# A chunked recurrence in a four-layer block: five elementwise steps moved to GpSimd, the 16x16 inverse built from two 8x8 ones, one root per group, and another order of the pieces

## The chip, the cores and the metric

The kernel runs on one core of a Trainium2 chip. The core has five engines that run side by side, each with an instruction queue worked off in order: TensorE (PE; its weight loads are shown apart as PEld), VectorE (DVE), ScalarE (ACT), GpSimd (POOL) and SyncE (SP, which issues most DMAs). Engines wait for each other by semaphores only. The metric is the device time of one execution in microseconds, lower is better.

## What is computed

One sequence of 512 tokens, width 1024, goes through four layers: a recurrent mixer (RWKV-7), windowed attention, a gated spatial unit and gated linear attention, each followed by a gated feed-forward block, everything in float32. The change touches the first mixer alone. Its core, per head (16 heads of 64 columns):

```python
def step(state, inp):
    r_t, d_t, k_t, v_t, kk_t, a_t = inp
    sa = jnp.einsum('bhvk,bhk->bhv', state, kk_t)
    state = (state * d_t[:, :, None, :]
             - sa[..., None] * (kk_t * a_t)[:, :, None, :]
             + v_t[..., None] * k_t[:, :, None, :])
    return state, jnp.einsum('bhvk,bhk->bhv', state, r_t)
...
mean = jnp.mean(y, -1, keepdims=True)
var = jnp.mean(jnp.square(y - mean), -1, keepdims=True)
y = ((y - mean) * lax.rsqrt(var + RW_GN_EPS)).reshape(B, S, D) * gn_g + gn_b
bonus = (jnp.sum(hs(r) * hs(k) * r_k, -1, keepdims=True) * hs(v)).reshape(B, S, D)
return ((y + bonus).astype(x.dtype) * g) @ w_o
```

## The kernel before

**How it is put in order.** The kernel's code does not emit instructions; every call is recorded as an operation with a price (`price`), and a planner (`Program.run`) then hands the operations out greedily, engine by engine, inside a window of 700 recorded operations, earliest recorded first unless another can start much sooner. The result is one fixed order per engine. The planner also counts PE's work and, where PE would otherwise rest too long, puts in filler products of the identity with itself (line 525 of the profile). All real instructions carry line 239, the planner's `call`, so they are told apart by their tiles. What is recorded first, and at what price, thus sets the order; `ORDERS` says in which sequence the pieces of the recurrence are recorded.

**The recurrence.** It is done in chunks of 64 tokens (eight of them), in four groups of two column blocks of 128 (four heads a group). Each group goes through these pieces:

- *prepare* (`rwkv_prepare`, pieces `f` and `q`): decays by a scan over tokens, keys, receptances. It writes `qk` (what is multiplied by the state) and `kb` (what goes into it), whose tiles are called `qk`, `h` or `rk` according to the group; temporaries are `ew` and `et` (`slot` for the first group). Two of its steps are `kn * kf[p]` (tile `ew<-ew,rk`) and the outer part of `qk`, receptance times decay (`qk<-rk,et` and alike).
- *products* (`rwkv_products`, first half of the pieces `p`): the 64x64 products of keys with keys and receptances per chunk and head, masked on their way out of PSUM into `pr` or `pa`; beside it `kb` is multiplied by the chunk's whole decay `pend`.
- *inverse* (`rwkv_inverse`, the other pieces `p`): 64x64 triangular blocks are inverted. ACT collects their 16x16 diagonal blocks on the partitions (`et` or `slot`), DVE turns them by a 32x32 transpose, solves column by column (15 steps, each a product and a sum over the last axis, of i*i elements in step i), and turns back. Two levels of PE products, ACT masks (`low`) and DVE transposes and sums (`mt`) then make 32x32 and 64x64 inverses (`iv`). `rwkv_direct` folds them into `qk`.
- *chain* (`rwkv_chain`, pieces `c`): four blocks of two chunks. In each chunk PE multiplies `qk` by the state `st`, ACT copies the result (`vu`), PE makes the chunk's contribution to the state, and DVE adds it to the decayed state (`st<-ps,wu`, two halves). This is serial from chunk to chunk. Each second block ends with ACT's copy of `y` (tile `out`).
- *out* (`rwkv_out`, pieces `o`, one for each half of the tokens): mean, variance and `rsqrt` (eleven small DVE instructions, tiles `gvar`, `grs`, `rs_t`), the bonus on POOL (`out<-v,bonus`), transposes, gate, and the split for the output projection.

The pieces of group n's chain are recorded between those of the inverse of group n + 1 and the preparation of later groups. `pr` and `pa` have one buffer each, so the products of group n + 2 wait for the chain of group n. The first group's preparation and inverse are recorded beside the projection of the values (PE `whi,slot` and `wlo,slot`, dense work); the output projection (`et,rk`) follows the last group, and its first part is done beside it. From there on PE is dense through the rest of the program. The lines of the inverse's steps:

```python
for i in range(1, 16):
    w = tmp[:, :i * i].rearrange("p (j m) -> p j m", j=i)
    nc.vector.tensor_mul(w, n1[:, i, :i].unsqueeze(1).to_broadcast([P, i, i]), t4[:, 0, :i, :i])
    nc.vector.tensor_reduce(t4[:, 0, :i, i], w, axis=AX.X, op=ALU.add)
nc.scalar.copy(t4[:, 1], t4[:, 0])
nc.vector.transpose(n, tt)
```

Of the kernel before, what the change touches and what calls it, by code (L numbers as in the profile page):

```python
# [29 lines left out]
ALSO = {"exp": ("tanh",), "sigmoid": ("tanh",), "silu": ("sin", "tanh"), "gelu": ("tanh",)}  # L30
ORDERS = "ffppcpqcpqqcopcopcoo", "ppcpqcpqqcopcopcoo", "ppcpcpcopcopcoo", "cccococ"
LOCAL = "qqqqqaqaqaqaoaoooaoaoaoo"
# [474 lines left out]
class K:  # L507
# [509 lines left out]
    def rwkv(self, g, g_next, slots):  # L1017
# [5 lines left out]
        nc, d = self.nc, self.d  # L1023
# [14 lines left out]
        v = self.v = self.load_cols()  # L1038
# [197 lines left out]
    def part(self, name, dt=F32, w=S):  # L1236
        p = self.pl[name]
        return p.tile([P, w], dt, name="slot" if p is self.big else name)

    def rwkv_prepare(self, sb, rf, kf, twa, keep, sel, rs, ka1):  # L1240
# [18 lines left out]
        for i, p in enumerate(sb['pairs']):  # L1259
# [41 lines left out]
    def rwkv_products(self, sb, hf):  # L1301
# [6 lines left out]
        for i in range(2):  # L1308
# [12 lines left out]
    def rwkv_inverse(self, sb):  # L1321
# [16 lines left out]
        nc.vector.transpose(n, zx)  # L1338
        n2, t4 = n.rearrange("p (t b m) -> p t b m", t=16, b=2), tt.rearrange("p (j b i) -> p b j i", j=16, b=2)
        n1 = zx[:, :256].rearrange("p (t m) -> p t m", t=16)  # L1340
# [140 lines left out]

    def rwkv_out(self, sb, hf, y, tg):

        nc = self.nc
        H, W = 8, 256
        hd = lambda t: t.rearrange("p (h c) -> p h c", h=H)
        bc = lambda t, n=H: t.unsqueeze(2).to_broadcast([P, n, 64])
        mean, var, rs = [self.sm.tile([P, H], F32, name=n) for n in ("gmean", "gvar", "grs8")]
        sq, bv = self.part("out"), self.part("out")
        for j in range(2):  # L1490
            b = hf * 2 + j
            bo = sb['bonus'][:, b].rearrange("p g h -> p (g h)")
            four = lambda t: t.rearrange("p (h c) -> p h c", h=4)
            nc.gpsimd.tensor_mul(four(bv[:, j * W:(j + 1) * W]), four(sb['v'][b]), bc(bo, 4))
        nc.vector.tensor_reduce(mean, hd(y), axis=AX.X, op=ALU.add)
        nc.vector.tensor_scalar(mean, mean, 1.0 / 64, None, op0=ALU.mult)
        nc.vector.tensor_sub(hd(y), hd(y), bc(mean))
        nc.scalar.activation(sq, y, AF.Square)
        nc.vector.tensor_reduce(var, hd(sq), axis=AX.X, op=ALU.add)
        nc.vector.tensor_scalar(var, var, 1.0 / 64, 64e-5, op0=ALU.mult, op1=ALU.add)  # L1500
        self.rsqrt(rs, var)
        nc.vector.tensor_mul(hd(y), hd(y), bc(rs))
        yt, bt, gt = [self.bank() for _ in range(3)]
# [499 lines left out]
def consts():  # L2003
# [10 lines left out]
    f = np.arange(S)  # L2014
    eye = np.broadcast_to((f // 32 == f % 16).astype(np.float32), (P, S)).copy()
    return {'rw_masks': masks, 'rw_eye': eye, 'rope_freq': freq}
# [129 lines left out]
```

## Time and profile before

| what | us |
|---|---|
| median of three runs (2392.96 to 2395.63) | 2394.17 |
| profiled execution, first to last instruction (its span) | 2393.6 |
| PE busy in it | 2352.7 |
| DVE busy in it | 1934.0 |
| ACT busy in it | 1437.0 |
| POOL busy in it | 326.3 |

The profiled execution is one of its own; its span of 2393.6 us stands 0.6 us below the median of the runs, and no other time is known of it. Times inside the program are counted from its first instruction. PE's busy time includes the time that a product takes from start to end, also where a next one could start earlier, so a busy PE is not one at its peak. "Idle before, released by" names the instruction whose semaphore came last.

The first group's inverse ends at about 205 us, the chains of the four groups end at about 256, 304, 350 and 391 us, and the output projection ends at about 431 us.

### The profile page before, as it was taken

Reading aid. Unit: us, or ns where it says so; the run is one execution under the profiler, and the core shown is the slowest. Engines: PE = TensorE matmul, PEld = TensorE weight load, DVE = VectorE, ACT = ScalarE, POOL = GpSimd, SP = SyncE. Lnnn points to the kernel's source line nnn. Section 1 sums busy time; section 2 is a strip of 40 time slices with the busy share of each in tenths; the row PEclk is TensorE's granted clock in tenths of the full one; section 3 lists DMA queues with packets and bytes.
Section 4 is the critical chain, followed back from the end, with each engine's and each line's share of the span. In section 5 each row is a group of like instructions: output and inputs, shape, how many; then the busy total and the mean of one; then the engine's idle time right before and its main releaser. Section 6 shows DMA issues by size and latency. Waiting matters only on the chain.

```text
span 2393.6 us, 36634 instructions
## 1 busy us (share of the span) xinstructions
PE 2352.7 (98%) x13524; PEld 1925.6 (80%) x13524; DVE 1934.0 (81%) x3261; ACT 1437.0 (60%) x2514; POOL 326.3 (14%) x398
## 2 busy tenths in 40 slices
PE   9999889999999999999999999999999999999998
PEld 8577777988888769888887888888888778988886
DVE  8577987887889878878699888886869978886868
ACT  4476765755556587555575444755557737755555
POOL 0000000221211001211111101121121101121110
PEclk9999999999999999999999999999999999999999
DMA  5220012998998326999988664899898758899985
GB/s 174 71 77 13 8 66 65 214 217 221 220 213 202 88 65 156 211 234 217 215 217 212 187 157 100 197 210 227 219 216 210 166 134 171 203 204 233 218 207 118
DMA packets 127603, 404.23 MB, mean 169 GB/s; under 512 B 14400, under 2 KB 17984, under 8 KB 127424
## 3 DMA queue, kind: packets, MB, share of 16 engines
q0 software_dynamic: 51840, 176.18, 41.2%
q1 hardware_dynamic: 75584, 225.72, 28.1%
q8 instruction: 106, 1.74, 0.3%
q14 instruction: 73, 0.60, 0.1%
HBM read 397.39 MB, written 2.10 MB: 167 GB/s over the span
## 4 chain that ended last, share of the span: by engine, by line
PE 83%; DVE 6%; ACT 5%; DMA 4%; issue 2%; SPq 0%; POOL 0%; DVEq 0%; ACTq 0%; POOLq 0%
PE ps L239 83%; DVE slot L239 2%; ACT slot L239 2%; DMA wraw<-ffn_w_a 2%; DMA wraw<-ffn_w_b 1%; DVE wlo L239 1%; ACT et L239 1%; ACT whi L239 1%; DVE h L239 1%; ACT vu L239 0%; ACT wu L239 0%; DMA wraw<-sg_w_o 0%; ACT L239 0%; DVE left L239 0%; DMA slot<-x 0%
## 5 line engine op out<-in xcount | busy, mean ns | idle before, releaser
L239 PE MATMUL ps<-whi,slot 128*128 128x512 f32 (+1 forms) x5072 | 1554.2, 384 | 3.6 <-DVE slot L239 3.1
L239 PEld LDWEIGHTS ps<-whi,slot 128*128 128x128 f32 x5072 | 943.3, 188 | 179.2 <-ACT whi L239 8.0
L239 ACT CAST whi<-wraw 128x1024 fp32r<-128x1024 f32 (+3 forms) x843 | 688.3, 836 | 565.4 <-PE ps L239 432.9
L239 DVE TENSOR_TENSOR wlo<-wraw,whi 128x1024 fp32r<-128x1024 f32 (+3 forms) x843 | 790.5, 954 | 256.6 <-ACT whi L239 254.8
L239 PE MATMUL ps<-wlo,slot 128*128 128x512 f32 (+1 forms) x2536 | 968.9, 382 | 1.8 <-DVE wlo L239 1.8
L239 PEld LDWEIGHTS ps<-wlo,slot 128*128 128x128 f32 x2536 | 476.5, 188 | 86.5 <-DVE wlo L239 6.6
L239 PE MATMUL ps<-slot,whi 128*128 128x512 f32 x688 | 217.1, 395 | 1.0 <-ACT slot L239 1.0
L239 DVE TENSOR_TENSOR slot<-ps,slot 128x512 f32<-128x512 f32 (+2 forms) x271 | 161.0, 608 | 48.4 <-PE ps L239 33.9
L239 ACT CAST slot<-left 128x512 fp32r<-128x512 f32 (+1 forms) x294 | 164.6, 589 | 53.4 <-PE ps L239 29.5
L239 DVE TENSOR_TENSOR slot<-left,slot 128x512 fp32r<-128x512 f32 (+1 forms) x294 | 183.4, 644 | 10.8 <-ACT slot L239 6.9
L239 DVE TENSOR_TENSOR h<-h,ps 128x512 f32<-128x512 f32 x240 | 159.7, 683 | 27.7 <-PE ps L239 25.2
L239 POOL DMA_DIRECT2D wraw<-ffn_w_a x128 | 109.7, 860 | 497.8 <-DVE wlo L239 415.1
L239 PEld LDWEIGHTS ps<-slot,whi 128*128 128x128 f32 x688 | 127.7, 188 | 32.7 <-DVE slot L239 2.6
L239 PE MATMUL ps<-slot,wlo 128*128 128x512 f32 x344 | 133.9, 391 | 0.0
L239 POOL DMA_DIRECT2D wraw<-ffn_w_b x64 | 54.9, 864 | 419.9 <-DVE slot L239 119.9
L239 ACT COPY slot<-ps 128x512 f32<-128x512 f32 (+1 forms) x144 | 78.4, 562 | 39.0 <-PE ps L239 36.9
L239 POOL DMA_DIRECT2D wraw<-ffn_o_a x64 | 54.6, 853 | 285.6 <-DVE wlo L239 151.9
L239 ACT COPY left<-ps 128x512 f32<-128x512 f32 x108 | 54.8, 558 | 57.0 <-PE ps L239 57.0
L239 PE MATMUL ps<-ident,slot 128*128 128x128 f32 x561 | 85.8, 277 | 0.9 <-DVE slot L239 0.6
L239 PEld LDWEIGHTS ps<-ident,slot 128*128 128x128 f32 x561 | 63.3, 140 | 26.0 <-DVE slot L239 12.9
L239 PEld LDWEIGHTS ps<-slot,wlo 128*128 128x128 f32 x344 | 64.5, 188 | 14.2 <-DVE wlo L239 0.8
L239 DVE SCALAR_TENSOR_TENSOR slot<-slot,ncol 128x512 f32<-128x512 f32 (+1 forms) x96 | 65.1, 701 | 9.2 <-ACT slot L239 9.0
(302 smaller groups left out, 2070.2 us busy)
## 6 DMA issues: line engine op xcount, KB each, us to landing
wraw<-ffn_w_a SPq DMA_DIRECT2D x128, 512.0 KB, 6.6
wraw<-ffn_w_a POOLq DMA_DIRECT2D x128, 512.0 KB, 6.9
wraw<-ffn_o_a SPq DMA_DIRECT2D x64, 512.0 KB, 5.1
wraw<-ffn_o_a POOLq DMA_DIRECT2D x64, 512.0 KB, 7.3
wraw<-ffn_w_b SPq DMA_DIRECT2D x64, 384.0 KB, 3.9
wraw<-ffn_w_b POOLq DMA_DIRECT2D x64, 384.0 KB, 6.4
wraw<-gla_w_p SPq DMA_DIRECT2D x24, 512.0 KB, 4.9
wraw<-gla_w_p POOLq DMA_DIRECT2D x24, 512.0 KB, 6.3
```

What stands on the lines that cost most here:

```text
L239: op = self.add(eng.name, lambda: getattr(eng.target, what)(*map(real, args), **{k: real(a) for k, a in kw.items()}), *self.price(eng.name ...
```

## The change

Five products leave DVE for POOL: `kn * kf[p]`, the outer part of `qk`, the decay of `kb`, and the subtraction of the mean (two, two, four and two instructions a group). The 16x16 solve becomes two 8x8 solves in one (seven steps over both diagonal blocks), then two 512-element products with a sum each for the block below; ACT's copy now writes both transposed copies, 512 elements, and the table of ones that starts the solve has another layout. For the first three groups both halves of the tokens share one root; the last group keeps one for each half. The strings in `ORDERS` are permuted.

```diff
-ORDERS = "ffppcpqcpqqcopcopcoo", "ppcpqcpqqcopcopcoo", "ppcpcpcopcopcoo", "cccococ"
+ORDERS = "ffppcpqpqqccopcpocoo", "ppcpqcqppqcocopcoo", "pcpcppcpcoopcoo", "ccccooc"
...
-            out = (self.rwkv_out(sb, hf, sb['y'][hf], tg) for hf in range(2))
+            out = self.rwkv_norm(sb, tg, ((0, 1),) if n < 3 else ((0,), (1,)))
...
-            nc.vector.tensor_mul(kn, kn, kf[p])
+            nc.gpsimd.tensor_mul(kn, kn, kf[p])
...
-            nc.vector.tensor_mul(outer(qk), nat(rf[p]), nat(e))
+            nc.gpsimd.tensor_mul(outer(qk), nat(rf[p]), nat(e))
...
-            nc.vector.tensor_mul(kb, kb, sb['pend'][:, i, hf * 4:hf * 4 + 4].unsqueeze(2).to_broadcast([P, 4, P]))
+            nc.gpsimd.tensor_mul(kb, kb, sb['pend'][:, i, hf * 4:hf * 4 + 4].unsqueeze(2).to_broadcast([P, 4, P]))
...
-        for i in range(1, 16):
-            w = tmp[:, :i * i].rearrange("p (j m) -> p j m", j=i)
-            nc.vector.tensor_mul(w, n1[:, i, :i].unsqueeze(1).to_broadcast([P, i, i]), t4[:, 0, :i, :i])
-            nc.vector.tensor_reduce(t4[:, 0, :i, i], w, axis=AX.X, op=ALU.add)
-        nc.scalar.copy(t4[:, 1], t4[:, 0])
-        nc.vector.transpose(n, tt)
+        for i in range(1, 8):
+            w = n[:, :2 * i * i].rearrange("p (q j m) -> p q j m", q=2, j=i)
+            nc.vector.tensor_mul(w, nq[:, :, i, :i].unsqueeze(2).to_broadcast([P, 2, i, i]), tq[:, :, :i, :i])
+            nc.vector.tensor_reduce(tq[:, :, :i, i], w, axis=AX.X, op=ALU.add)
+        w = n.rearrange("p (j i m) -> p j i m", j=8, i=8)
+        eights = [P, 8, 8, 8]
+        nc.vector.tensor_mul(w, n1[:, 8:, :8].unsqueeze(1).to_broadcast(eights), t1[:, :8, :8].unsqueeze(2).to_broadcast(eights))
+        nc.vector.tensor_reduce(x1, w, axis=AX.X, op=ALU.add)
+        nc.vector.tensor_mul(w, t1[:, 8:, 8:].rearrange("p m i -> p i m").unsqueeze(1).to_broadcast(eights), x1.unsqueeze(2).to_broadcast(eights))
+        nc.vector.tensor_reduce(t1[:, :8, 8:], w, axis=AX.X, op=ALU.add)
+        nc.scalar.copy(tmp.rearrange("p (j b i) -> p j b i", j=16, b=2), t1.unsqueeze(2).to_broadcast([P, 16, 2, 16]))
+        nc.vector.transpose(n, tmp)
...
+    def rwkv_norm(self, sb, tg, turns):
...
+        for turn in turns:
+            var, rs = [self.sm.tile([P, 2 * H], F32, name=n)[:, :H * len(turn)] for n in ("gvar", "grs8")]
...
+                nc.vector.tensor_reduce(mean, hd(y), axis=AX.X, op=ALU.add)
+                nc.vector.tensor_scalar(mean, mean, 1.0 / 64, None, op0=ALU.mult)
+                nc.gpsimd.tensor_sub(hd(y), hd(y), bc(mean))
+                nc.scalar.activation(sq, y, AF.Square)
+                nc.vector.tensor_reduce(part(var, j), hd(sq), axis=AX.X, op=ALU.add)
+                if hf != turn[-1]:
+                    yield
+            nc.vector.tensor_scalar(var, var, 1.0 / 64, 64e-5, op0=ALU.mult, op1=ALU.add)
+            self.rsqrt(rs, var)
+            for j, hf in enumerate(turn):
+                nc.vector.tensor_mul(hd(sb['y'][hf]), hd(sb['y'][hf]), bc(part(rs, j)))
+                self.rwkv_out(sb, hf, tg)
+            yield
```

What moves on the engines: every engine's order is the same up to the first group's preparation and again from the output projection on; between them it is planned anew. PE, at the end of the value projection, where the first group's levels begin (`slot,pa` and `slot,low` are the two levels of its inverse, `h` the next group's products, L525 the fillers), before:

```order
L239 MATMUL ps<-whi,slot 128x512
L239 MATMUL ps<-ident,qk 128x128 x4
L239 MATMUL ps<-ew,sel 32x128 x4
L239 MATMUL ps<-h 128x128 x12
L525 MATMUL ps<-ident 128x128 x4
L239 MATMUL ps<-slot,pa 64x64 x32
L525 MATMUL ps<-ident 128x128 x2
L239 MATMUL ps<-slot,low_1209 64x64 x16
L239 MATMUL ps<-slot,low_1224 64x64 x16
L525 MATMUL ps<-ident 128x128 x4
L239 MATMUL ps<-slot,pa 64x64 x32
```

and now:

```order
L239 MATMUL ps<-wlo,slot 128x512
L239 MATMUL ps<-whi,slot 128x512
L239 MATMUL ps<-slot,pa 64x64 x32
L239 MATMUL ps<-whi,slot 128x512
L239 MATMUL ps<-slot,low_1209 64x64 x16
L239 MATMUL ps<-slot,low_1224 64x64 x16
L239 MATMUL ps<-wlo,slot 128x512
L239 MATMUL ps<-whi,slot 128x512
L239 MATMUL ps<-ew,sel 32x128 x4
L239 MATMUL ps<-h 128x128 x3
L239 MATMUL ps<-slot,pa 64x64 x32
```

The fillers are gone from there, the last value products and the next group's products stand between the levels. DVE, at the end of the second group's solve, before:

```order
L239 TENSOR_TENSOR et<-et 128x196
L239 TENSOR_TENSOR ew<-ew,rk 128x512
L239 TENSOR_REDUCE et<-et 128x14
L239 TENSOR_TENSOR rk<-ew,et 128x4x2x64
L239 TENSOR_TENSOR et<-et 128x225
L239 SCALAR_TENSOR_TENSOR ew<-rk,vec,ew 128x512
L239 TENSOR_REDUCE et<-et 128x15
L239 TENSOR_TENSOR rs_t<-grs_2440 128x8
L239 TENSOR_TENSOR st_1175<-ps,wu 64x2x64
```

and now:

```order
L239 TENSOR_TENSOR et<-et 128x98
L239 TENSOR_TENSOR st_1197<-ps,wu 64x2x64
L239 TENSOR_REDUCE et<-et 128x2x7
L239 TENSOR_TENSOR et<-et 128x512
L239 TENSOR_REDUCE gmean<-out 128x8
L239 TENSOR_REDUCE et<-et 128x64
L239 TENSOR_TENSOR st_1175<-ps,wu 64x2x64
L239 TENSOR_TENSOR et<-et 128x512
L239 TENSOR_TENSOR st_1175<-ps,wu 64x2x64
L239 TENSOR_REDUCE et<-et 128x8x8
```

The long tail of growing steps has become two pairs of 512 elements, and the chain's additions still stand between the steps. POOL, in the second and third group, had the bonus alone before:

```order
L239 TENSOR_TENSOR out<-v_1360,bonus 128x256
L239 TENSOR_TENSOR out<-v_1375,bonus 128x256
L239 TENSOR_TENSOR out<-v_1421,bonus 128x256
L239 TENSOR_TENSOR out<-v_1435,bonus 128x256
L239 TENSOR_TENSOR out<-v_1666,bonus 128x256
```

and now:

```order
L239 TENSOR_TENSOR ew<-ew,rk 128x512
L239 TENSOR_TENSOR out<-out,gmean 128x512
L239 TENSOR_TENSOR rk<-rk,pend 128x512 x4
L239 TENSOR_TENSOR out<-v_1362,bonus 128x256
L239 TENSOR_TENSOR out<-v_1376,bonus 128x256
L239 TENSOR_TENSOR out<-v_1424,bonus 128x256
L239 TENSOR_TENSOR out<-v_1438,bonus 128x256
L239 TENSOR_TENSOR qk<-rk,et 128x4x2x64
L239 TENSOR_TENSOR out<-out,gmean 128x512
L239 TENSOR_TENSOR ew<-ew,rk 128x512
```

Forty instructions of 512 elements have joined POOL's queue, which works them off in order. ACT's queue has one table load (`ACT_TABLE_LOAD`) more, at the last group's preparation.

More of the change, by code (lines that the diff above doesn't have):

```diff
@@ L1338, in rwkv_inverse @@
         nc.vector.transpose(n, zx)
[L1339 to L1340 removed]
+        n2 = n.rearrange("p (t b m) -> p t b m", t=16, b=2)
+        n1, t1, x1 = [t.rearrange("p (t m) -> p t m", m=m) for t, m in ((zx[:, :256], 16), (tt[:, :256], 16), (tt[:, 272:336], 8))]
         nc.vector.tensor_add(n1, n2[:, :, 0, :], n2[:, :, 1, :])
[L1342 to L1347 removed]
+        nq, tq = [t[:, :272].rearrange("p (q x) -> p q x", q=2)[:, :, :P].rearrange("p q (t m) -> p q t m", t=8) for t in (zx, tt)]
+        for i in range(1, 8):
[10 more added lines that the diff above has]
+        nc.vector.transpose(n, tmp)
         tu = n.rearrange("p (j x u) -> p u x j", j=16, x=2)
@@ L1480, in rwkv_chain @@
             yield
-    def rwkv_out(self, sb, hf, y, tg):
+    def rwkv_norm(self, sb, tg, turns):
         nc = self.nc
-        H, W = 8, 256
+        H = 8
         hd = lambda t: t.rearrange("p (h c) -> p h c", h=H)
-        bc = lambda t, n=H: t.unsqueeze(2).to_broadcast([P, n, 64])
-        mean, var, rs = [self.sm.tile([P, H], F32, name=n) for n in ("gmean", "gvar", "grs8")]
-        sq, bv = self.part("out"), self.part("out")
+        bc = lambda t: t.unsqueeze(2).to_broadcast([P, H, 64])
+        for turn in turns:
+            var, rs = [self.sm.tile([P, 2 * H], F32, name=n)[:, :H * len(turn)] for n in ("gvar", "grs8")]
+            part = lambda t, j: t[:, j * H:(j + 1) * H]
+            for j, hf in enumerate(turn):
+                y, sq, mean = sb['y'][hf], self.part("out"), self.sm.tile([P, H], F32, name="gmean")
+                nc.vector.tensor_reduce(mean, hd(y), axis=AX.X, op=ALU.add)
[7 more added lines that the diff above has]
+            self.rsqrt(rs, var)
+            for j, hf in enumerate(turn):
+                nc.vector.tensor_mul(hd(sb['y'][hf]), hd(sb['y'][hf]), bc(part(rs, j)))
+                self.rwkv_out(sb, hf, tg)
+            yield
@@ L1490, in rwkv_out @@
+    def rwkv_out(self, sb, hf, tg):
+        nc, y = self.nc, sb['y'][hf]
+        W = 256
+        bv = self.part("out")
         for j in range(2):
-            b = hf * 2 + j
-            bo = sb['bonus'][:, b].rearrange("p g h -> p (g h)")
             four = lambda t: t.rearrange("p (h c) -> p h c", h=4)
-            nc.gpsimd.tensor_mul(four(bv[:, j * W:(j + 1) * W]), four(sb['v'][b]), bc(bo, 4))
-        nc.vector.tensor_reduce(mean, hd(y), axis=AX.X, op=ALU.add)
-        nc.vector.tensor_scalar(mean, mean, 1.0 / 64, None, op0=ALU.mult)
@@ L1497, in rwkv_out @@
[L1497 to L1502, printed above, removed]
+            bo = sb['bonus'][:, hf * 2 + j].rearrange("p g h -> p (g h)")
+            nc.gpsimd.tensor_mul(four(bv[:, j * W:(j + 1) * W]), four(sb['v'][hf * 2 + j]), bo.unsqueeze(2).to_broadcast([P, 4, 64]))
@@ L2014, in consts @@
     f = np.arange(S)
-    eye = np.broadcast_to((f // 32 == f % 16).astype(np.float32), (P, S)).copy()
+    eye = np.broadcast_to((f // 16 == f % 16).astype(np.float32), (P, S)).copy()
     return {'rw_masks': masks, 'rw_eye': eye, 'rope_freq': freq}
```

## The prediction

> **What bounds the kernel now.** The page comes first: PE is busy nearly all the time, so a change that adds no dense work can only save time where PE is not doing any.
>
> ```profile
> span 2393.6 us, 36634 instructions
> PE 2352.7 (98%) x13524; PEld 1925.6 (80%) x13524; DVE 1934.0 (81%) x3261; ACT 1437.0 (60%) x2514; POOL 326.3 (14%) x398
> ```
>
> Next the busy times by stretch, cut where the chains of the four groups end (columns after the stretch's length: PE, PEld, DVE, ACT, POOL, then the granted clock).
>
> ```profile
> 165.00:205.00 40.00, 39.16 (x450) 33.20 (x446) 29.26 (x66) 20.45 (x34) 2.37 (x4) 1.00 0.09 28
> 205.00:258.00 53.00, 47.51 (x689) 34.49 (x680) 47.50 (x120) 44.97 (x93) 0.00 (x0) 0.94 0.05 15
> 258.00:305.00 47.00, 40.91 (x688) 33.63 (x686) 43.87 (x124) 33.00 (x78) 2.58 (x4) 1.00 0.04 10
> 305.00:352.00 47.00, 41.53 (x823) 34.96 (x819) 39.10 (x119) 32.31 (x78) 4.82 (x8) 1.00 0.23 79
> 352.00:393.00 41.00, 40.47 (x610) 32.00 (x607) 30.45 (x77) 24.73 (x63) 0.00 (x0) 1.00 0.08 26
> ```
>
> The three stretches from 205 to 352, one for each of the first three chains (I call them loops), are the only ones where PE rests visibly: 17.05 of 147 us, and its weight loads, which leave out the tails of small products, fill only 103.1 us. DVE is busy 47.5, 43.9 and 39.1 us there, 130.5 of 147 (89%), more than any other engine does work. In the fourth stretch the output projection fills PE, so nothing in it can save much; what comes after is ordered as before. The saving must come from the three loops and from the end of the stretch before them.
>
> Who waits in the loops:
>
> ```profile
> PEld ps L239 <- ACT vu L239: 15.2, 19, 1.6
> PEld ps L239 <- DVE st L239: 4.6, 13, 1.0
> ```
>
> That is the serial chain: PE's weight loads wait for ACT's copy `vu` and for DVE's state. And the chain of waits followed back through the loops, by shares:
>
> ```profile
> by line: PE ps L239 39.4%; ACT et L239 13.1%; ACT vu L239 6.3%; ACT wu L239 6.2%; issue 4.0%; ACT ew L239 3.3%; ACT L239 2.6%; PE ps L525 2.6%; DVE out L239 2.6%; ACT out L239 2.3%; DVE st L239 2.3%; DVE et L239 2.2%; DVE pr L239 2.0%; DVE
> ```
>
> The two views disagree: by busy time DVE is the bound, on the chain of waits its named rows are 9.1%, and with all that is cut off (11.1%) at most 20%. So a microsecond of DVE saved is worth between 0.2 and 0.89 us. That span is the main doubt of this forecast.
>
> **First term: the end of the value projection.** PE before the loops, from the timeline:
>
> ```profile
> 193.06 1.16 PE L525 MATMUL ps<-ident 128*128 128x128 f32 x8
> 194.64 2.08 PE L239 MATMUL ps<-slot,pa 64*64 64x64 f32 x64 [0.42 <-DVE slot L239]
> 196.65 0.71 PE L525 MATMUL ps<-ident 128*128 128x128 f32 x4
> 197.29 2.08 PE L239 MATMUL ps<-slot,low 64*64 64x64 f32 x64
> 199.31 1.16 PE L525 MATMUL ps<-ident 128*128 128x128 f32 x8
> 200.88 2.08 PE L239 MATMUL ps<-slot,pa 64*64 64x64 f32 x64 [0.42 <-DVE slot L239]
> ```
>
> PE has nothing but fillers from 193.06 to 194.64, 196.65 to 197.29 and 199.31 to 200.88: 3.79 us. In the new order these three places hold value products and products `h`, which cost nothing extra. For that the first solve must end sooner, which the terms below give it (some 3 us of DVE). A third I leave for products that are themselves late: **-2.5 us** (between -3.8 and 0).
>
> **Second term: work that leaves DVE in the loops.** The moved instructions there:
>
> ```profile
> L239 DVE TENSOR_TENSOR ew<-ew,rk 128x512 f32<-128x512 f32 x5 | 3.4, 682 | 0.0
> L239 DVE TENSOR_TENSOR qk<-rk,et 128x512 f32<-128x512 f32 x2 | 1.4, 684 | 0.0
> L239 DVE TENSOR_TENSOR rk<-rk,et 128x512 f32<-128x512 f32 x2 | 1.4, 681 | 0.0
> L239 DVE TENSOR_TENSOR h<-rk,et 128x512 f32<-128x512 f32 x1 | 0.7, 680 | 0.0
> L239 DVE TENSOR_TENSOR rk<-rk,pend 128x512 f32<-128x512 f32 x4 | 2.7, 684 | 0.2 <-PE ps L239 0.2
> L239 DVE TENSOR_TENSOR qk<-qk,pend 128x512 f32<-128x512 f32 x4 | 2.7, 682 | 0.0
> L239 DVE TENSOR_TENSOR h<-h,pend 128x512 f32<-128x512 f32 x3 | 2.1, 688 | 0.3 <-PE ps L239 0.2
> L239 DVE TENSOR_TENSOR out<-out,gmean 128x512 f32<-128x512 f32 x5 | 3.4, 685 | 0.0
> ```
>
> 26 instructions, 17.8 us. The other 14 of the forty lie under dense PE work before 205 or after 352, and count for nothing: PE is busy 39.2 of 40 and 40.5 of 41 us there.
>
> The solve, in the loops (three groups), with two of its products and what a 512-element sum and a strided read cost:
>
> ```profile
> L239 DVE TENSOR_TENSOR et<-et 128x256 f32<-128x256 f32 (+15 forms) x48 | 12.5, 261 | 0.8
> L239 DVE TENSOR_REDUCE et<-et 128x1 f32<-128x1 f32 (+14 forms) x45 | 10.5, 234 | 0.4
> L239 DVE TENSOR_TENSOR et<-et 128x49 f32<-128x49 f32 x1 | 0.2, 204 | 0.0
> L239 DVE TENSOR_TENSOR et<-et 128x225 f32<-128x225 f32 x1 | 0.4, 398 | 0.0
> L239 DVE TENSOR_REDUCE gmean<-out 128x8 f32<-128x512 f32 x6 | 4.1, 678 | 0.0
> L239 DVE TENSOR_TENSOR mt<-et,mk 128x256 f32<-128x256 f32 x12 | 6.3, 588 | 0.0
> ```
>
> 49 and 225 elements at 204 and 398 ns give 150 + 1.1 n ns. Before: 23.0 us less three additions of 256 elements (0.43 each), 21.7, or 7.2 a group in 30 instructions. Now seven products of 2, 8, 18, 32, 50, 72 and 98 elements (280): 7 x 150 + 1.1 x 280 = 1.36 us; their sums at most as much; two sums of 512 at 0.68; one product at 0.68, and one that reads in steps of 16 elements. For that the row `mt<-et,mk` stands (steps of 32): 588 against 432 by the formula, 0.31 us more for 512 elements, 0.99. Together 5.75 us in 18 instructions: 1.45 us a group, 4.4 us in the loops.
>
> The root:
>
> ```profile
> L239 DVE TENSOR_TENSOR rs_t<-grs 128x8 f32<-128x8 f32 x15 | 2.7, 180 | 0.0
> L239 DVE SCALAR_TENSOR_TENSOR grs<-rs_t,grs 128x8 f32<-128x8 f32 x15 | 2.3, 155 | 0.0
> L239 DVE SCALAR_TENSOR_TENSOR rs_t<-gvar,rs_t 128x8 f32<-128x8 f32 x15 | 2.3, 152 | 0.1
> ```
>
> Five roots, 7.3 us, 1.46 each; the six of the first three groups become three: 4.4 us. Eight columns more cost 8 x 1.1 ns. DVE is thus relieved of 17.8 + 4.4 + 4.4 = 26.6 us.
>
> **Third term: what POOL takes back.** POOL's price, and the one place in the loops where DVE is held up beside it:
>
> ```profile
> 343.84 1.27 POOL L239 TENSOR_TENSOR out<-v,bonus 128x256 f32<-128x256 f32 x2 [14.03 <-PE ps L239]
> 343.93 0.71 DVE L239 TENSOR_TENSOR et<-et 128x169 f32<-128x169 f32 x1
> 344.56 0.57 DVE L239 TENSOR_TENSOR rs_t<-grs 128x8 f32<-128x8 f32 x1
> ```
>
> Two products of 256 elements take POOL 1.27 us, so one of 512 takes about 1.25, against 0.68 on DVE. 26 of them are 32.5 us in 147, beside the twelve of 256 (7.4 us) that it has: POOL is not full, but queues in order. The two DVE rows should take 0.34 (by the formula) and 0.18 us; they took 0.37 and 0.39 longer and ended as POOL's did. Both read two SBUF tiles, and so do POOL's. The stall is 0.76 us for the loops' twelve POOL instructions, 0.06 each. With instructions twice as long it is at least 0.13 us for each of the 26, 3.4 us; at most DVE stands for what is left of 1.25 us after a short instruction or two, 0.9, or 23.4 us. About half of DVE's instructions in the loops read two SBUF tiles, but the four on `pend` stand beside masks that read PSUM. I take 0.3, nearer the measured end: 8 us. The Trainium skill (SBUF — State Buffer, "Who interferes with whom") says that a VectorE instruction with two SBUF inputs and a GpSimd instruction that reads SBUF shut each other out for their whole length. These two rows agree; by that rule alone the stall would go towards the upper end, 23.4 us, and the second term would be all but gone.
>
> **Net.** Relief of DVE in the loops: 26.6 - 8 = 18.6 us. Between 0.2 and 0.89 I take 0.55, the middle, since neither view has the better claim: **-10.2 us**.
>
> **Small terms.** On ACT, in the loops:
>
> ```profile
> L239 ACT COPY et<-et 128x256 f32<-128x256 f32 x3 | 1.2, 406 | 1.7 <-DVE et L239 1.7
> L239 ACT ACT_TABLE_LOAD x4 | 5.1, 1283 | 0.1
> ```
>
> The copy stands between the solve and DVE's turn and grows from 256 to 512 elements: between 0 and 0.4 us more, I take 0.2 in each of three groups, **+0.6**. One table load more costs nothing while ACT rests 14 us in that loop; uncovered it would be 1.3. PE's clock has one hole in the loops:
>
> ```profile
> 226.00:230.00 4.00, 1.77 (x32) 1.18 (x33) 3.26 (x7) 3.88 (x10) 0.00 (x0) 1.00 0.00 0
> 230.00:237.00 7.00, 6.80 (x86) 5.10 (x82) 5.41 (x23) 6.01 (x16) 0.00 (x0) 0.51 0.00 0
> ```
>
> After 4 us with PE busy 1.77 the granted clock is 0.51 for 7 us, 3.4 us of clock lost. Whether the new order keeps this hole, closes it or adds others no row shows: -3.4 if it closes, +3.4 for each new one, 0 taken.
>
> The mean's subtraction and the shared root make each half's output later; nobody but the output projection waits for it, and its first products come a loop later. POOL's queue puts `ew<-ew,rk` and the receptances behind the `pend` products, which wait for PE; late next are DVE's `kb` and the products of the following group.
>
> **Sum.** -2.5 - 10.2 + 0.6 = -12.1 us, a span of 2381.5; with the 0.6 us by which the runs' median stands above the span, 2382.1. I give 2382. Likeliest range: coupling 0.2 with 0.9 of the first term gives -5.4, coupling 0.89 with the stall at 8 us -18.5: 2375 to 2389.
>
> **The rivals.** *DVE is the bound throughout:* its 89% and idle times of 3 to 8 us a loop speak for it, the chain's 20% against. With the low stall, 23.2 x 0.89 + 3.8 = 24.4 us less: 2370. *The serial chain sets the pace, and the relief turns into DVE's idle time:* the 15.2 us for `vu` speak for it; the first term and the longer copy are left, 2392. Three new holes in PE's clock beside the forecast's gain end there too: 10.2 of 12.1 us gone. *POOL's products come onto the path:* `kn * kf`, the receptances' decay, the `pend` products and the mean each have a waiting instruction behind them; if each of 26 shows its extra length (1.25 - 0.68) and DVE's stalls come to the upper 23.4 us, the sum is -2.5 - 0.55 x 3.2 + 0.6 + 26 x 0.57 = +11.1, 2405. It decides, slower by more than 0.2%, once 15 of the 26 are on the path. Against it: most prepare a later group.
>
> **How the numbers follow.** Some 0.2%, 4.8 us, is what a measurement of this kernel tells from no change: below 2389.4 is faster, above 2399 slower. Forecast 0.60, DVE throughout 0.14, chain sets the pace or clock holes 0.15, POOL on the path 0.11 (0.03 of it ends within 0.2%). Faster is 0.60 + 0.14 + 0.03 of the chain case = 0.77, same 0.12 + 0.03 = 0.15, slower 0.08. The range takes in DVE throughout and the chain case: 2369 to 2393.
>
> **What would show it.** Right: no L525 rows between the first group's levels; `et<-et` in the loops near 17 us instead of 23; DVE about 110 to 120 us over the three loops; fourth stretch unchanged near 41 us. The port: DVE products with two SBUF inputs, `rk<-et,ew` or `ew<-ew,et`, longer than 0.69 us by some tenths in the mean. Wrong: loops as long as before with DVE's idle grown (chain), a granted clock below 0.94 in a loop (holes), or PE and DVE waiting for POOL by several us (POOL on the path).

## The result, and the profile after

The changed kernel takes 2417.48 us (median of 2413.1 to 2419.31) against 2394.47 for the kernel before on the same chip: a ratio of 1.0093, 95% interval 1.0081 to 1.0104. By this ratio it is slower by 22.3 us (the two medians lie 23.0 apart; differences between runs go by the ratio from here on). 2382 was forecast, and slower had a chance of 0.08. Its profiled execution spans 2416.4 us.

Head of the page after:

```profile
span 2416.4 us, 36518 instructions
PE 2362.3 (98%) x13508; PEld 1933.0 (80%) x13508; DVE 1929.1 (80%) x3140; ACT 1439.1 (60%) x2515; POOL 378.3 (16%) x438
```

By stretch, cut at the ends of the four chains as before (columns: length, then PE, PEld, DVE, ACT, POOL, granted clock, and DMA):

```profile
165.00:205.00 40.00, 37.65 (x447) 30.80 (x443) 28.10 (x51) 22.36 (x35) 6.37 (x6) 1.00 0.08 28
205.00:271.00 66.00, 53.81 (x862) 42.39 (x862) 51.62 (x95) 48.86 (x102) 18.96 (x15) 0.90 0.04 12
271.00:325.00 54.00, 45.85 (x756) 37.05 (x756) 43.72 (x96) 33.49 (x78) 12.20 (x12) 1.00 0.03 10
325.00:367.00 42.00, 37.11 (x491) 29.86 (x492) 31.81 (x75) 28.67 (x70) 9.92 (x12) 0.88 0.24 84
367.00:407.00 40.00, 39.89 (x675) 31.08 (x674) 27.57 (x71) 24.08 (x61) 3.27 (x4) 1.00 0.07 24
```

The three loops take 162 us instead of 147. DVE works 127.2 us in them instead of 130.5, so its idle time has grown from 16.5 to 34.8 us. PE rests 25.2 instead of 17.1 us, and its clock is at 0.90 and 0.88 in two of the loops. The output projection ends at 447.8 instead of 430.8 us, 17.0 of the 22.8 us by which the span grew; the rest lies later (the clock is at half once more, 504 to 510 us).

What PE lost up to there can be told in two numbers. Before and after, from 165 us to the end of the output projection:

```profile
165.00:430.80 265.80, 246.87 (x3402) 197.81 (x3398) 222.79 (x560) 175.70 (x389) 11.65 (x18) 0.99 0.16 49
165.00:447.80 282.80, 254.57 (x3412) 203.38 (x3408) 217.29 (x447) 179.85 (x390) 53.66 (x52) 0.96 0.15 47
```

PE rests 18.9 us before and 28.2 after: +9.3. Where the trace has PE at half clock, half of its busy time is lost: 3.3 us before, 10.6 after: +7.3. Together 16.6 of 17.0. A third sum is what the planner's fillers take of PE, 12.1 us before and 10.5 after. The table below has the three sums for every run.

**DVE beside POOL.** The two engines in the second group's preparation, DVE first:

```profile
243.13 0.62 DVE L239 COPY rk<-et 128x8 f32<-128x8 f32 x1
243.66 0.68 DVE L239 SCALAR_TENSOR_TENSOR rk<-et,ew 128x512 f32<-128x512 f32 x1
244.27 1.60 DVE L239 TENSOR_TENSOR mt<-et,mk 128x256 f32<-128x256 f32 x1
245.78 1.71 DVE L239 TENSOR_TENSOR rk<-ew,et 128x512 f32<-128x512 f32 x1
247.53 1.63 DVE L239 SCALAR_TENSOR_TENSOR ew<-rk,vec,ew 128x512 f32<-128x512 f32 x1
```

```profile
241.93 1.79 POOL L239 TENSOR_TENSOR ew<-ew,rk 128x512 f32<-128x512 f32 x1 [20.13 <-ACT ew L239]
243.68 1.79 POOL L239 TENSOR_TENSOR rk<-rk,et 128x512 f32<-128x512 f32 x1
245.43 1.52 POOL L239 TENSOR_TENSOR ew<-ew,rk 128x512 f32<-128x512 f32 x1
246.90 1.71 POOL L239 TENSOR_TENSOR rk<-rk,et 128x512 f32<-128x512 f32 x1
```

`mt<-et,mk` takes 1.60 us for 0.59, `rk<-ew,et` 1.71 for 0.68, and POOL's own products 1.5 to 1.8 for 1.27: by these rows each engine stands while the other works. Summed over the rows of DVE from 205 to 367 us that are longer than the same form undisturbed (25 rows, without the 0.9 us of the new strided products), it is 15.8 us beside 41 us of POOL. No wait shows it: one row of the view of waits names POOL as the one waited for, with 0.2 us. The hold is inside the instruction's length.

**The chain's addition.** The sixth chunk of the first chain: PE's product for the state ends, then DVE adds. PE and DVE before, from the timelines (the seventh chunk beneath, the longest wait of that chain before):

```profile
240.84 0.45 PE L239 MATMUL ps<-vu,tok 128*64 128x64 f32 x8
...
244.79 0.45 PE L239 MATMUL ps<-vu,tok 128*64 128x64 f32 x8 [0.34 <-ACT vu L239]
```

```profile
241.62 0.28 DVE L239 TENSOR_TENSOR st<-ps,wu 64x128 f32<-64x128 f32 x1
...
248.44 0.28 DVE L239 TENSOR_TENSOR st<-ps,wu 64x128 f32<-64x128 f32 x1
```

and the sixth chunk after:

```profile
245.67 0.40 PE L239 MATMUL ps<-vu,tok 128*64 128x64 f32 x8
```

```profile
255.51 0.69 DVE L239 TENSOR_TENSOR mt<-mt,ps 128x512 f32<-128x512 f32 x1 [2.26 <-PE ps L239]
...
258.63 0.75 DVE L239 SCALAR_TENSOR_TENSOR ew<-rk,vec,ew 128x512 f32<-128x512 f32 x1
259.30 0.58 DVE L239 TENSOR_TENSOR st<-ps,wu 64x128 f32<-64x128 f32 x2
```

Before, DVE adds 0.3 us after the product in the sixth chunk and 3.2 us in the seventh; now it adds 13.2 us after the product in the sixth. In the new plan that addition stands behind other work of DVE, and behind the first level of the next inverse, for which DVE itself waits for PE (2.26 us). The chain's last copy starts at 269.6 instead of 256.4 us, and the products of the third group, which write the tile that the first chain reads (`pa`, one buffer), are masked from 274.0 instead of 260.6 us.

### The profile page after: what moved, and what is told of

Same layout as the page of the kernel before. It is cut to its first block, busy times and chain, and to the rows that moved or that the text cites. A ratio compares the mean times of both kernels' runs of the same rounds, so it can differ in the third digit from the quotient of the medians.

```text
span 2416.4 us, 36518 instructions
## 1 busy us (share of the span) xinstructions
PE 2362.3 (98%) x13508; PEld 1933.0 (80%) x13508; DVE 1929.1 (80%) x3140; ACT 1439.1 (60%) x2515; POOL 378.3 (16%) x438
## 4 chain that ended last, share of the span: by engine, by line
PE 82%; DVE 8%; ACT 5%; DMA 2%; issue 2%; POOL 0%; SPq 0%; DVEq 0%; ACTq 0%; POOLq 0%
PE ps L239 82%; ACT slot L239 2%; DVE slot L239 2%; DVE wlo L239 1%; DMA wraw<-ffn_w_b 1%; DVE h L239 1%; ACT whi L239 1%; DMA wraw<-ffn_o_a 1%; ACT et L239 0%; DVE ew L239 0%; ACT L239 0%; ACT wu L239 0%; DMA wraw<-sg_w_o 0%; ACT vu L239 0%; DVE pa L239 0%
## 5 line engine op out<-in xcount | busy, mean ns | idle before, releaser
L239 PEld LDWEIGHTS ps<-wlo,slot 128*128 128x128 f32 x2536 | 477.3, 188 | 91.0 <-DVE wlo L239 10.7
L239 PEld LDWEIGHTS ps<-ident,slot 128*128 128x128 f32 x561 | 63.9, 141 | 25.9 <-DVE slot L239 12.7
```

Source lines behind the costliest of these rows:

```text
L239: op = self.add(eng.name, lambda: getattr(eng.target, what)(*map(real, args), **{k: real(a) for k, a in kw.items()}), *self.price(eng.name ...
```

## The experiments

Two theories stood at the start: POOL's products carry the loss (their length and their hold on DVE), or the new order of the work does. A third came from the clock: rests of PE that bring half-clock stretches. "Kept plan" means that the planner is told nothing of the edit, so that PE's and ACT's rows, and all others where possible, stand in the same order; "planned anew" means that it is.

The table has each run against the kernel before on the same chip (change and 95% interval in per cent; 0.1% is 2.4 us), and from its trace, from 165 us to the end of the output projection: when that ends, PE's rest, the loss by half clock, PE's time in fillers (a filler at half clock counts in both), and how long the chain's state waited for DVE at the longest in the first loop (product's end to the start of its addition; in e12, where other rows stand between the two halves of one addition, to the second half).

| run | change, interval | ends | rest | half clock | fillers | addition |
|---|---|---|---|---|---|---|
| before | | 430.8 | 18.9 | 3.3 | 12.1 | 3.2 |
| after | +0.93 (0.81, 1.04) | 447.8 | 28.2 | 10.6 | 10.5 | 13.2 |
| e1 after's plan, 32 products cut | +0.23 (0.12, 0.33) | 433.5 | 22.0 | 5.0 | 10.5 | 11.0 |
| e2 after's plan, products on DVE | +0.84 (0.69, 0.99) | 449.5 | 28.2 | 13.5 | 11.5 | 11.8 |
| e3 before's plan, products on POOL | +0.30 (0.18, 0.43) | 438.4 | 19.8 | 10.0 | 12.4 | 3.6 |
| e4 moves undone, planned anew | +0.68 (0.53, 0.83) | 442.3 | 23.1 | 8.2 | 15.2 | 10.0 |
| e5 solve alone, planned anew | +0.68 (0.49, 0.88) | 441.6 | 24.7 | 5.0 | 13.7 | 10.7 |
| e6 root alone, planned anew | +0.32 (0.19, 0.45) | 436.6 | 19.3 | 5.1 | 14.8 | 3.1 |
| e7 piece order alone | +1.00 (0.82, 1.18) | 453.5 | 22.7 | 10.1 | 24.5 | 13.8 |
| e8 after with the old piece order | +0.93 (0.78, 1.08) | 451.2 | 26.4 | 13.4 | 14.4 | 10.9 |
| e9 solve, before's plan | +0.33 (0.21, 0.46) | 441.9 | 22.3 | 11.4 | 14.2 | 2.0 |
| e10 a price 10 ns higher | +0.05 (-0.03, 0.14) | 431.5 | 17.7 | 5.0 | 12.4 | 3.2 |
| e11 after, fillers in PE's rests | +0.64 (0.51, 0.78) | 446.1 | 20.1 | 6.4 | 21.6 | 11.3 |
| e12 after, POOL priced as traced | +1.21 (1.07, 1.35) | 460.0 | 27.2 | 17.8 | 18.5 | 15.1 |
| e13 solve spread, before's plan | +0.11 (0.02, 0.20) | 432.6 | 21.1 | 3.4 | 12.4 | 4.2 |
| e14 before's plan, 32 products cut | -0.11 (-0.20, -0.02) | 428.4 | 17.2 | 3.3 | 12.0 | 2.7 |
| e15 before without fillers | +0.16 (0.06, 0.25) | 436.1 | 27.0 | 12.7 | 0.0 | 3.2 |
| e16 moves alone, planned anew | +1.00 (0.86, 1.14) | 458.6 | 25.2 | 19.7 | 18.0 | 16.1 |

**POOL or DVE, at a kept plan (e1, e2, e3, e4).** A second name for an engine records work for one engine in the plan and issues it on another:

```diff
+        self.lent = Engine(self, "POOL", nc.vector)   # e2; e3: "DVE", nc.gpsimd
-            nc.gpsimd.tensor_mul(kn, kn, kf[p])       # and the four others
+            nc.lent.tensor_mul(kn, kn, kf[p])
```

e1 cuts three of the five products to 8 columns each at their old price and leaves the other columns out; e4 puts `nc.vector` back in the code.

> The changed kernel with its order kept on every engine, but 32 of the 40 products that moved to POOL (kn * kf, the pend products, the mean) now work on 8 of their 512 columns; the planner still prices them as whole ones, and the growing decay in the keys is set to one so that the values stay finite. Left out: what the other columns would have been multiplied by. Every wait, place and dependency stays, only POOL's time and its hold on DVE go. If POOL's products carry the loss (late results, and the 16 us by which DVE rows in 205 to 367 us are longer beside them), the time falls by 15 us or more, to 2385 to 2402. If the order of the pieces carries it, it stays at 2412 or above.

> The changed kernel planned as it is, with PE's and ACT's orders the same row by row, but the forty products that moved to POOL are issued by DVE at the same places of the plan. DVE has 27 us of work more, and no row of it is stretched by those products any more (16 us in 205 to 367). If POOL's lateness and its hold on DVE cost more than the relief of DVE is worth, 2400 to 2414; if the relief was real and the order costs the time, 2420 to 2430.

> The kernel before with its plan, PE's and ACT's orders the same row by row, but the forty products are issued by POOL at the same places of the plan: the move alone, without a new order, the solve or the root. If POOL's products carry the loss, 2402 to 2415; if the order carries it, 2385 to 2398.

> The changed kernel with the five moves undone in the code and planned anew: 8x8 solves, one root a group and the new piece order stay. If POOL's products carry the loss, it is faster than before by what the solve, the root and the fillers were forecast at: 2.5 + 0.55 x 8.8 - 0.6 = 6.7 us, 2384 to 2391. If the new order of the pieces carries it, 2408 to 2420.

e1 took 2401.14, e2 2414.81, e3 2401.66, e4 2412.57, against 2395.30 for before. Neither theory holds alone. With 32 products all but gone the changed plan is still 5.5 us above before: that is the plan, the solve and the root. With them it is 22.3 us above: 16.8 us for products. Putting them back on DVE in that plan changes little (e2), so POOL gives back what DVE is spared. And undoing the moves leaves 16.3 us (e4). The move alone, in before's plan, costs 7.2 us (e3), with DVE's rows longer by 14.7 us. So 7.2 of the 22.3 us are the move at the old order, and 15.1 come with the new plan, the solve and the root.

**Each part alone (e5 to e8, e16).** Each is the code of before with one hunk of the change, e8 the code after with `ORDERS` of before.

> The kernel before with the two 8x8 solves alone, planned anew. The forecast's own term for it: 4.4 us of DVE at 0.55, 0.6 back for the copy, so 2393.5 against 2395.3, within what is told from no change. If a plan made anew costs by itself whatever changes in it, 2400 to 2415.

> The kernel before with the shared root alone (the first half's output waits for the second half's variance), planned anew. By the forecast's term 4.4 us of DVE at 0.55: 2393. If the shared root carries the 17 us that the kernel with the moves undone lost, by holding back the first half's output and its buffers until the second half's last block, 2405 to 2415.

> The kernel before with the permuted piece order alone, planned anew. If the piece order carries the 17 us, 2405 to 2415; if the root or the solve does, 2392 to 2400.

> The changed kernel with the piece order of before and everything else kept: five moves, 8x8 solves, one root. If the piece order carries most of the loss, what is left is the price of the moves seen at a kept order (6 us) less the gain of the solve and the root: 2393 to 2403. If the root carries it, 2410 to 2420.

> The kernel before with the five moves to POOL alone, planned anew. At the kept plan they cost 6.4 us. If the planner finds as good a place for them, 2399 to 2404; if a plan made anew for another set of instructions costs 8 to 18 us more, as with the root and the solve alone, 2408 to 2420.

They took 2411.5, 2401.73, 2417.65 and 2416.7 against 2393.74, and 2419.66 against 2394.57. Every part alone costs 8 to 24 us once it is planned anew, the piece order as much as all together, and the old piece order does not mend the changed kernel. The parts do not add up; what they share is a new plan. In e7 some half of the 22.7 us by which the output projection ends later are fillers: the planner put in 24.5 us of them instead of 12.1. In all but the root's the chain's addition waits 10 to 16 us for DVE (3.2 before). In e16, PE's product and DVE's addition:

```profile
254.07 0.45 PE L239 MATMUL ps<-vu,tok 128*64 128x64 f32 x8 [1.38 <-ACT vu L239]
```

```profile
258.49 4.04 DVE L239 TENSOR_TENSOR mt<-et,mk 128x256 f32<-128x256 f32 x4
...
268.00 0.68 DVE L239 TENSOR_TENSOR mt<-mt,ps 128x512 f32<-128x512 f32 x1
...
270.59 0.28 DVE L239 TENSOR_TENSOR st<-ps,wu 64x128 f32<-64x128 f32 x1
```

The same products on the same engine in before's plan (e3) cost 7.2 us, in a plan of their own 23.9: the plan is 16.7 of it.

**A plan made anew for nothing, and a better price (e10, e12).**

```diff
-            slow = 90.0 if views[0].buf.name.startswith("st") else ...
+            slow = 100.0 if views[0].buf.name.startswith("st") else ...      # e10
-        return max(150.0, 37.0 + n * (0.83 ... else 2.4)), 250.0
+        return max(150.0, 37.0 + n * (0.83 ... else 3.4)), 250.0             # e12
```

> The kernel before with nothing changed in what is computed or on which engine; the planner alone is told that an instruction that writes the state takes 10 ns more (100 for 90 in that part of the price). Some rows of the recurrence then change places (about 110 lines on PE, 135 on DVE). If a plan made anew costs by itself, because the plan of before is one of the better draws, 2399 to 2412. If only the particular piece order, solve or root cost, within 2 us of before.

> The changed kernel planned anew with POOL's products priced at 1.78 us instead of 1.27, as the trace shows them beside DVE. If the planner's wrong price of POOL is why the new plan is slow, 2400 to 2410; if any plan for this set of instructions is slow until its piece order is found by trial, 2410 to 2425.

e10 took 2396.73, e12 2424.98, against 2395.15. A small shuffle costs nothing that can be told, so not every new plan is bad. And the truer price made the plan worse by 7 us than the wrong one; the half clock takes 17.8 us there and the fillers 18.5. The addition waits here too, in the fifth chunk, where the two halves of the state are added far apart. PE and DVE in e12:

```profile
239.60 0.45 PE L239 MATMUL ps<-vu,tok 128*64 128x64 f32 x8
```

```profile
240.59 0.28 DVE L239 TENSOR_TENSOR st<-ps,wu 64x128 f32<-64x128 f32 x1
...
255.11 0.29 DVE L239 TENSOR_TENSOR st<-ps,wu 64x128 f32<-64x128 f32 x1
```

The second half is added 15.1 us after the product's end, and PE makes the next chunk's product at 264.06 us. How much of a plan's loss the waiting addition makes is not shown: no run puts it alone back in its place. In e1 it waits 11.0 us, and the whole run is 5.5 us above before.

**The solve in the old places (e9, e13).** The 30 old instructions stay in the plan; what is issued at their places is exchanged:

```diff
+        for i, op in enumerate(places):
+            op.call = steps[i] if i < len(steps) else lambda: None        # e9; e13 spreads the 18 over the 30
```

> The kernel before with its plan kept row by row on PE, ACT, POOL and SP; only the solve is exchanged: the 18 instructions of the two 8x8 solves stand in the first 18 of the 30 places of the old solve, the other twelve places are empty, and ACT's copy is the longer one. If the forecast's term was right and the plan made anew was what cost 17.8 us in the run with the solve alone, it gains 0.9 to 3.9 us, less 0.6 for the copy: 2391 to 2395. If the solve itself costs (the longer copy, the strided product), 2400 or more.

> As the run with the solve in the kept plan, but its 18 instructions stand spread evenly over the 30 old places, the last in the last one, so that no long step is pulled in front of other work of DVE. If pulling the long steps forward held up DVE's other work, the time comes back to 2391 to 2396; if the loss comes through the half clock that any shift of the row of work may bring, 2398 to 2408.

e9 took 2404.68 against 2395.15, e13 2397.65 against 2394.57. In e9 the 512-element steps stand where short ones stood, and the split of a weight of the value projection, for which PE waits, comes 2 us later: DVE before and in e9 (there the solve has line 1344):

```profile
183.45 1.22 DVE L239 TENSOR_TENSOR wlo<-wraw,whi 128x1024 fp32r<-128x1024 f32 x1
```

```profile
183.62 0.68 DVE L1344 TENSOR_TENSOR slot<-slot 128x512 f32<-128x512 f32 x1
...
184.82 0.68 DVE L1344 TENSOR_REDUCE slot<-slot 128x64 f32<-128x512 f32 x1
185.42 1.22 DVE L239 TENSOR_TENSOR wlo<-wraw,whi 128x1024 fp32r<-128x1024 f32 x1
```

From there everything runs some 2 us later, and three more half-clock stretches follow (8.1 us). Spread over the old places the loss falls to 2.6 us. No run shows a gain from the shorter solve.

**What relief of DVE is worth (e14).** Before's plan row by row, 32 products on DVE cut to 8 columns, nothing put elsewhere:

```diff
-            nc.vector.tensor_mul(kn, kn, kf[p])
+            nc.vector.tensor_mul(kn, kn, kf[p]).call = self.late(nc.vector, "tensor_mul", one(kn), one(kn), one(kf[p]))
```

> The kernel before with its plan kept row by row on every engine; of the 40 products in question 32 (kn * kf, the pend products, the mean) stay on DVE but work on 8 of their 512 columns, the growing decay set to one so that values stay finite. Left out: the other columns. It takes about 0.5 us from each, 16 us of DVE, some 11 of them in the three loops, and adds nothing anywhere. By the forecast's coupling of 0.55 it gains 5 to 7 us, 2388 to 2391; if the relief turns into idle time of DVE because the serial chain sets the pace, 2393 to 2397; if earlier ends move PE's rests into more half-clock stretches, 2398 to 2408.

It took 2392.39 against 2394.57. Its loops:

```profile
205.00:257.00 52.00, 47.43 (x681) 34.79 (x683) 43.55 (x119) 45.13 (x94) 0.00 (x0) 0.93 0.05 15
257.00:304.00 47.00, 41.30 (x723) 34.60 (x720) 41.54 (x126) 33.54 (x80) 2.37 (x4) 1.00 0.04 10
304.00:350.00 46.00, 41.00 (x796) 34.33 (x792) 35.41 (x116) 31.72 (x76) 4.82 (x8) 1.00 0.24 82
```

From 205 us to the end of the third chain DVE works 118.1 us for 128.4 (10.3 less) in 142.6 us for 144.9 (2.3 less); its idle time grows by 8.0. A microsecond taken off DVE is worth 0.22 in this trace; by the interval of the run's time (0.5 to 4.8 us gained) it is 0.05 to 0.47.

**The clock (e11, e15, e17, e18).** e11 issues 45 more fillers ahead of eight instructions of PE, by hand and unknown to the planner; e15 leaves out the 39 fillers of the recurrence; e17 and e18 hold four copies on ACT back.

```diff
+                if k in self.HOLES[op.names]:
+                    self.warm[1](self.HOLES[op.names][k])      # e11
+            if 54 <= self.nc.fills < 93: return                 # e15
```

> The changed kernel with its order kept, and 45 filler products more in front of eight PE instructions that waited 1 to 3.3 us in its trace (ahead of the second group's bonus products, the first levels of the inverses, and others). They use time in which PE rests; if the half-clock stretches behind those rests are what is lost there (10.6 us of PE time in 165 to 448, against 3.3 before), the time falls by 3 to 7 us, to 2410 to 2414. If the clock is beside the point, 2416 to 2422.

> The kernel before with its plan kept, but the 39 filler products of the recurrence (between 140 and 400 us) left out. They are some 11 us of PE's busy time. If the plan of before stands near the half clock, more stretches of it appear and the time rises by 5 to 20 us, 2400 to 2415; if the clock were beside the point, the time stays or falls, 2386 to 2396.

> The kernel before with one swap on ACT: in the second group, the last four copies that collect the inverse's blocks (et<-pr, 224.1 to 227.0) stand behind the copy tok (226.96) instead of ahead of it. PE's rest from 224.9 to 227.6 shrinks or splits, the solve begins 0.6 us later. If the half-clock stretch from 230 to 237 goes and was a cause, 2390 to 2393; if it stays or the serial chain sets the pace, 2394 to 2396; if the later solve counts in full, 2395 to 2396.

> The same swap, with the four copies behind tok and the three chain copies that follow it (wu twice, vu), so that the chain goes on 2.8 us sooner and the solve begins 1.7 us later. If chain and clock set the time, 2388 to 2392; if the inverse does, 2395 to 2397.

e11 took 2412.08 against 2395.15, 5 to 7 us less than the changed kernel, as the clock theory said, but not where it said: up to the output projection PE's rest fell by 8.1 us and the half clock by 4.2, the fillers took 11.1 more, and 1.7 us were gained; the rest is that the half-clock stretch at 504 us, in a part that is ordered alike, is missing from its trace. e15 took 2398.83 against 2394.57: 12.1 us of fillers saved, 8.1 more of rest and 9.4 more of half clock. So the fillers hold the clock, at about what they cost. e17 (2395.27) and e18 (2396.05, both against 2395.23) tell nothing apart: the rest only split in two of 1.7 us, and the half-clock stretch behind it stayed (229 to 236 us). A kernel that beats both was not found; e14 leaves work out.

## Why the prediction was wrong, by its own steps

**First term, -2.5: not there, -0.4 at most.** The fillers did go from the end of the value projection, as forecast. But PE rests there for a split that DVE makes later:

```profile
187.36 0.60 PE L239 MATMUL ps<-ident,qk 128*128 128x128 f32 x4
190.31 0.50 PE L239 MATMUL ps<-wlo,slot 128*128 128x512 f32 x1 [2.35 <-DVE wlo L239]
```

The last step of the first inverse starts at 204.5 us, 204.9 before.

**Second term, 26.6 us of relief: the rows right, their worth not.** The solve and the roots after, in the loops:

```profile
L239 DVE TENSOR_TENSOR et<-et 128x512 f32<-128x512 f32 (+9 forms) x32 | 13.0, 406 | 0.8
L239 DVE TENSOR_REDUCE et<-et 128x64 f32<-128x512 f32 (+7 forms) x27 | 8.1, 301 | 0.7
L239 DVE SCALAR_TENSOR_TENSOR grs<-rs_t,grs 128x16 f32<-128x16 f32 x6 | 2.3, 387 | 0.1
L239 DVE TENSOR_TENSOR rs_t<-grs 128x16 f32<-128x16 f32 x6 | 1.7, 278 | 0.0
L239 DVE SCALAR_TENSOR_TENSOR rs_t<-gvar,rs_t 128x16 f32<-128x16 f32 x6 | 1.6, 269 | 0.1
```

Without the three additions (1.3 us together) and two splits (1.3 us together) of the same name the solve takes 18.5 us, 17.4 without POOL's hold, where 17.3 was forecast; the strided product takes 0.99 to 1.02 us, estimated at 0.99. The roots take 5.6, or 3.0 without the hold, for 2.9. So the rows shrank by 26.4 us. But rows overlap: above, a product of 0.68 us that starts at 243.66 is followed by the next at 244.27. Up to the third chain's end DVE's rows add up to 147.0 us before, in 128.4 us of busy time, and to 136.8 after, in 126.0. Durations thus count 18.6 us twice before and 10.8 after, and 7.8 us of the relief were such overlap.

**Third term, the port: 8 us taken, 15.8 measured,** 15.0 of it for the 27 products in the loops, 0.56 each instead of 0.3, between the two bounds. The rule that was weighed (the Trainium skill, SBUF — State Buffer, "Who interferes with whom") held in kind: the masks `pa<-ps,mk`, which read PSUM, are 680 ns beside POOL or not; and the size lies nearer to its end than to the row I took. Relief, overlap and port together leave DVE 2.4 us less to do (126.0 for 128.4), not 18.6.

**The coupling: 0.55 taken, 0.22 measured (e14, 0.47 at most by its interval).** Two views disagreed, 0.2 by the chain of waits and 0.89 by busy time, and I took the middle. The chain of waits came nearer: DVE was busy 89% of the loops, and its work was mostly not on the path. The second and third term become -2.4 x 0.22 = -0.5 us instead of -10.2.

**The step that failed: that the order of everything else stays worth the same.** The sum has no term for it, nor a rival. With every term at its measured size it is -0.4 - 0.5 + 0.6 (the copy: 609 ns for 406, three times) = -0.3 us, and 22.3 were lost. By the runs the way from before to after is -2.6 (32 products gone, before's plan), +8.1 (after's plan, solve and root, those products still gone) and +16.8 (the products, on POOL, in that plan). In before's plan the products on POOL (all forty there) are 9.8 us dearer than gone (7.2 + 2.6). What of the 8.1 us the solve and the root would cost at the old order is known for the solve alone: 2.6 us with its steps spread over the old places (e13). The root alone was not run there. I compared the two orders at the places where the change's own instructions stand. The chain's addition, moved behind the inverse's levels, stood in the same list some rows further on, and it is an instruction that the change doesn't touch.

**Clock holes: 0 taken, +7.3 us.** The rival allowed three new ones, 3.4 us each; three more came up to the output projection, but the four last 23.9 us where the one lasted 6.8, and one more lies behind.

**The rivals.** *POOL on the path* (2405) came nearest in sign and size, but not by its mechanism: hardly anything waits for POOL; the port's hold, at two thirds of its upper end, and the plan make the loss. *The serial chain sets the pace* (2392) fits what e14 shows of the relief, most of which turns into idle time of DVE. That e14 took 2392.39 us is a coincidence: the rival's gain came from the first term, which is not there, and e14's from the little that the relief is worth. *DVE throughout* fell.

What stays open: seven of the nine plans that were made anew lost 16 us or more, and in all seven one addition of the first chain waits 10 to 16 us. In the other two, e6 and e10, it waits 3.1 and 3.2 us, and they lost 8 us and nothing that can be told. The two go together, but which part of a loss is the waiting addition's own was not taken apart, nor why e6 loses without one.

## What to carry to other kernels

Where a planner makes the order from prices, an edit of the work is an edit of the order: price the two apart, by issuing the new work at the old places, and follow in the new order the steps of the serial chain that the edit does not touch. Before an engine's relief is counted, take some of its work out at a kept order: 89% busy was worth 0.22 a microsecond here. And work given to GpSimd beside a busy VectorE is not off VectorE: it was held 0.56 us for each product, where a product of its own takes 0.60 from its start to the next one's.

## What the runs showed of the hardware

**PE's clock falls by windows, not by long rests.** The half-clock stretches are 3.4, 6.8, 10.2 or 13.7 us long, multiples of 3.41. I laid this grid over all twenty traces from 165 to 445 us and took the windows at full clock, 1,536. Where PE's matmuls were busy less than half of a window, the next was at half clock in 38 of 42 cases; from 0.5 to 0.7 in 17 of 85; from 0.7 to 0.9 in 6 of 323; above 0.9 in none of 1,086. Three pairs of such windows in the trace after:

```profile
213.50:216.90 3.40, 0.71 (x12) 0.38 (x10) 3.35 (x7) 2.44 (x3) 0.44 (x1) 0.99 0.00 0
216.90:220.30 3.40, 3.40 (x38) 3.31 (x31) 2.57 (x4) 2.52 (x6) 0.98 (x1) 0.50 0.02 5
227.10:230.50 3.40, 1.61 (x31) 1.13 (x31) 1.78 (x6) 3.35 (x8) 0.00 (x0) 1.00 0.01 2
230.50:233.90 3.40, 3.40 (x44) 2.78 (x42) 1.43 (x7) 2.99 (x8) 0.00 (x0) 0.50 0.02 5
244.20:247.60 3.40, 1.34 (x26) 1.08 (x26) 3.36 (x4) 1.98 (x7) 3.40 (x3) 1.00 0.00 0
247.60:254.40 6.80, 4.54 (x68) 4.16 (x70) 5.65 (x10) 0.63 (x2) 1.01 (x1) 0.50 0.00 0
```

PE rests 2.7 us ahead of the first stretch, 1.6 in one piece ahead of the second, and 1.0 and 1.1 in the third window (parts of rests of 1.9 and 3.3 us that reach beyond it). The Trainium skill (TensorE: Matmul & The Clock Gate, "HAM oscillation — how this bites in real kernels") gives the rule as no PE-idle gaps above some 3.4 us; here shorter ones brought the half clock, so the measurement is the stricter one.

**The same program varies by it.** In e5 the four runs took 2404.6, 2409.3, 2413.7 and 2414.4 us at mean granted clocks of 0.996, 0.995, 0.991 and 0.991, with one order and one amount of work. A rest of PE is thus often paid twice, and how often depends on where the windows fall.

**The hold between DVE and POOL takes short instructions hardest.** `pend<-et`, a copy of 8 columns, took 1305 ns beside POOL and 167 alone; a root's steps of 16 columns took up to 1031 for 168.
